# Low halves of the K and V weights: an accumulating DMA in place of a VectorE subtraction

## The chip, the cores and the metric

The kernel runs on one core of one Trainium2 chip. A core has TensorE (PE, matrix products), VectorE (DVE), ScalarE (ACT), GpSimd (POOL) and SyncE (SP), each with its own instruction stream, and 16 DMA engines that all queues share. The metric is the device time of one execution in microseconds. Three runs of the kernel before took 2151.91, 2154.38 and 2157.09 us; the median, 2154.38 us, is the time to compare with.

## The reference

One layer of a hybrid encoder over 256 tokens of width 2048, in float32:

```
h = x + W_out [ conv group || S5 group ] (rmsnorm(x))
h = h + MemCrossAttn(rmsnorm(h), rmsnorm(mem))      # 4 heads, 256 memory tokens
h = h + PEER(rmsnorm(h))                            # product-key experts
out = rmsnorm(h)

kv = (mem_n @ w_kv).reshape(bsz, 256, 2, 4, 512)    # w_kv is 2048 x 4096
k, v = kv[:, :, 0], kv[:, :, 1]
```

The change lies in the product with `w_kv`. Its first 2048 columns give K, the other 2048 give V.

## The kernel before

**How a weight product is made.** All large products go through one helper, `linear` (L146). It walks over blocks of 512 weight columns, and in each block over 8 tiles of 256 weight rows (`KG` = 2 groups of 128 rows). SP loads a tile of 512 KB into `w_raw` (L155). TensorE multiplies fast in the rounded format F32R, so each weight is taken apart into a high and a low half: ACT rounds the tile, `S.copy(hi, raw)` (L162), and DVE subtracts, `V.tensor_sub(lo, raw, hi)` (L163). TensorE then adds three products, high by high, high by low and low by high (L172 to L174 where tokens are the output rows, as for V; L181 to L183 where the output is transposed, as for K). For K this is 24 matmuls of 256 columns in a tile, for V 12 of 512 columns. The eighth tile of each block (`whole`) is not split: TensorE takes `w_raw` itself in float32 (L140, L143). So K and V have 64 tiles, 4 + 4 blocks of 8, and 56 of them are split.

**Buffers.** The pool `wp` has 5 buffers for `w_raw`, 3 for `w_hi` and 3 for `w_lo`. A buffer is used anew when its last reader is done, so a load waits for the split of the tile five before it, and a split waits for TensorE to be done with the tile three before it.

**What runs beside.** While K and V are made, the engines also run the S5 group (L428 to L469: table building on ACT, elementwise work and scans on DVE, small matmuls) and the depthwise convolution, 31 taps by 8 blocks of 128 channels, each tap one DVE instruction (L568). After V come the gated product of S5 (`ssm_glu_w`), the norms of the two groups and `w_out`.

**What sets the order.** Each engine runs its own stream strictly in order. The streams are laid out before the run by a scheduler that looks at priorities and at its own estimate of times: weight tiles are asked for `AHEAD` = 500 steps early and S5 bodies `S5_AHEAD` = 700 steps early, and the convolution fills the holes.

Of the kernel before, what the change touches and what calls it, by code (L numbers as in the profile page):

```python
# [9 lines left out]
F32 = mybir.dt.float32  # L10
# [4 lines left out]
AF = mybir.ActivationFunctionType  # L15
ALU = mybir.AluOpType
# [4 lines left out]
P = 128  # L21
T = 256
NTT = T // P
D = 2048
KT = D // P
# [3 lines left out]
PAD = CW - 1  # L29
KG = 2  # L30
AHEAD = 500
S5_AHEAD = 700
NPAIR = 32
NS = 64
# [26 lines left out]
W_IN, W_K, W_V = True, True, True  # L61
# [10 lines left out]
def trunk(ctx, tc, a, out, dbg=None):  # L72
    nc = tc.nc
    V, S, G, PE, SY = nc.vector, nc.scalar, nc.gpsimd, nc.tensor, nc.sync
# [45 lines left out]
    uctx = ctx.enter_context(ExitStack())  # L120
    with ExitStack() as wctx:
        atx = wctx.enter_context(ExitStack())
        wp = wctx.enter_context(tc.tile_pool(name="wp", bufs=3, side="right"))
        at = atx.enter_context(tc.tile_pool(name="at", bufs=1))
        psm = wctx.enter_context(tc.tile_pool(name="psm", bufs=3, space=PSUM))
        pst = wctx.enter_context(tc.tile_pool(name="pst", bufs=2, space=PSUM))
# [7 lines left out]
        def whole_matmuls(ps, x, raw, j, begin, end, rows_out):  # L134
            for i in range(KG):
                k = (j - (KT // KG - NWHOLE)) * KG + i
                first, last = begin and i == 0, end and i == KG - 1
                if rows_out:
                    for tt in range(NTT):
                        PE.matmul(ps[tt], x[:, k, tt * P:(tt + 1) * P], raw[:, i, :], start=first, stop=last)  # L140
                else:
                    for cb in range(4):
                        PE.matmul(ps[cb // 2][:, cb % 2, :], raw[:, i, cb * P:(cb + 1) * P], x[:, k, :],  # L143
                                  start=first and cb % 2 == 0, stop=last and cb % 2 == 1, skip_group_check=True)

        def linear(x, w, c0, ncol, evac, rows_out, kt=KT, korder=None, ahead=AHEAD, whole=None, cols=None):  # L146
            xh, xl = x
            js = korder or range(kt // KG)
            for n, (c, w_) in enumerate(cols or [(c, 512) for c in range(c0, c0 + ncol, 512)]):
                ncb = w_ // P  # L150
                ps = [psm.tile([P, 512] if rows_out else [P, 2, T], F32, name="mm", tag="mm") for _ in range(2)]
                for m, j in enumerate(js):
                    with tc.high_priority(offset=ahead):
                        raw = wp.tile([P, KG, w_], F32, name="w_raw", bufs=5)
                        SY.dma_start(raw, w[j * KG * P:(j + 1) * KG * P, c:c + w_].rearrange("(k p) c -> p k c", p=P))  # L155
                        full = whole is not None and j >= kt // KG - NWHOLE
                        if full:
                            whole_matmuls(ps, whole, raw, j, m == 0, m == len(js) - 1, rows_out)
                            continue
                        hi = wp.tile([P, KG, w_], F32R, name="w_hi")  # L160
                        lo = wp.tile([P, KG, w_], F32R, name="w_lo")
                        S.copy(hi, raw)  # L162
                        V.tensor_sub(lo, raw, hi.bitcast(F32))  # L163
                    for i in range(KG):
                        k = j * KG + i
                        first, last = m == 0 and i == 0, m == len(js) - 1 and i == KG - 1
                        ah, al = xh[k // 4][:, k % 4, :], xl[k // 4][:, k % 4, :]
                        if rows_out:
                            for tt in range(NTT):
                                o = ps[tt]  # L170
                                ts = slice(tt * P, (tt + 1) * P)
                                PE.matmul(o, ah[:, ts], hi[:, i, :], start=first, stop=False)  # L172
                                PE.matmul(o, ah[:, ts], lo[:, i, :], start=False, stop=False)  # L173
                                PE.matmul(o, al[:, ts], hi[:, i, :], start=False, stop=last)  # L174
                        else:
                            for cb in range(ncb):
                                o = ps[cb // 2][:, cb % 2, :]
                                end = cb % 2 == 1 or cb == ncb - 1
                                wh = hi[:, i, cb * P:(cb + 1) * P]
                                wl = lo[:, i, cb * P:(cb + 1) * P]  # L180
                                PE.matmul(o, wh, ah, start=first and cb % 2 == 0, stop=False, skip_group_check=True)  # L181
                                PE.matmul(o, wh, al, start=False, stop=False, skip_group_check=True)  # L182
                                PE.matmul(o, wl, ah, start=False, stop=last and end, skip_group_check=True)  # L183
                for half in range((ncb + 1) // 2):
                    evac(n, half, ps[half])
                yield n

        def run(g):
            for _ in g:
                pass  # L190
# [5 lines left out]
        with ExitStack() as mctx:  # L196
# [51 lines left out]
            def load_mem(src, gain):  # L248
                ssq = consts.tile([P, NTT, 4], F32, name="ssq_mem")
                x = act_tiles()  # L250
                xw = mp.tile([P, NWHOLE * KG, T], F32, name="x_whole")
                for n in range(4):
                    load_cols(src, None, ssq, n)
                r = row_rstd(ssq, "rstd_mem")
                for n in range(4):
                    xc, gb = load_cols(src, gain, None, n)
                    for tt in range(NTT):
                        V.scalar_tensor_tensor(xc[:, tt, :], xc[:, tt, :], r[:, tt:tt + 1], gb, op0=ALU.mult,
                                               op1=ALU.mult)
                    to_T(x, xw, n, xc)  # L260
                return x, xw

            def scaled(dst, ps, rb):
# [3 lines left out]

            uT = mp.tile([P, CQ, T], F32, name="uT")
            run(linear(xT, a["w_in"], 2 * CH, CH, lambda n, half, ps: V.tensor_mul(
                uT[:, 4 * n + 2 * half:4 * n + 2 * half + 2, :], ps, bc(rbx[:, None, :], [P, 2, T])), False, ahead=0))  # L270

# [201 lines left out]
            def s5_next():  # L473
                q = s5["q"]
                if q < CQ:
                  with tc.high_priority(offset=S5_AHEAD):
                    now = s5["tables"]
                    s5["tables"] = s5_tables(q + 1) if q + 1 < CQ else None
                    s5_body(q, now)
                    s5["q"] = q + 1  # L480

            for n in range(2):
                run(linear(xT, a["w_in"], n * 512, 512, ev_a(n), False, whole=xW if W_IN else None))
                s5_next()
                run(linear(xT, a["w_in"], CH + n * 512, 512, ev_g(n), False, whole=xW if W_IN else None))
                s5_next()
            memT, memW = load_mem(a["mem"], a["mem_norm_g"])
# [8 lines left out]
                S.copy(t, ps)  # L496
                SY.dma_start(v_dram[:, tt, 512 * n:512 * n + 512], t)

            for _ in linear(memT, a["w_kv_mem"], 0, D, ev_k, False, whole=memW if W_K else None):
                s5_next()  # L500
            kv_v = linear(memT, a["w_kv_mem"], D, D, ev_v, True, whole=memW if W_V else None)
            run(kv_v)
            for j in range(2):
                z = uT[:, 4 * j:4 * j + 4, :]
# [56 lines left out]
            for k in range(CW):  # L561
                for q in range(CQ):
                    src = cpad[:, q, k:k + T]
# [10 lines left out]
            for q in range(CQ):  # L574
                S.activation(acc[:, q, :], acc[:, q, :], AF.Silu, bias=colv[:, 2, q:q + 1],
                             scale=colv[:, 1, q:q + 1])
# [162 lines left out]
        for n in range((KD + 3) // 4):  # L739
            w = min(KD - 4 * n, 4)  # L740
# [384 lines left out]
```

## Time and profile before

| what | value |
|---|---|
| median of three runs | 2154.38 us |
| the profiled execution | 2160.26 us |
| its span in the trace | 2158.2 us |
| busy: PE, DVE, ACT, POOL | 92%, 82%, 48%, 35% of the span |
| K and V tiles | 64, of which 56 are split |

The profiled execution is 5.9 us longer than the median of the runs. The shares are averages over stages with different limits; what counts for this change is the stretch from about 220 to 460 us, in which K and V are made. Engine times in the trace are those of single instructions. PE's are modelled and overlap, so the pace of its matmuls is better read from how many stand in a stretch that it fills. A DMA has no line of its own in the table of instructions; its cost shows as the busy share of the 16 DMA engines and as pieces of the chain of waits.

### The profile page before, as it was taken

What the parts mean: (1) busy time and instruction counts of PE and PEld (TensorE: products, weight loads), DVE (VectorE), ACT (ScalarE), POOL (GpSimd) and SP (SyncE); (2) the same over time, 40 slices, a digit from 0 to 9 for tenths busy, and PEclk for the clock granted to TensorE, in tenths of its full rate; (3) what the DMA queues carried; (4) which work ended last, traced back from release to release, by engine and by line L of the source; (5) the groups of instructions that cost most, each with busy time, mean ns of one, the idle gap of its engine ahead of it and who ended that gap; (6) DMA issues with size and microseconds to landing.
All of it is one profiled execution on the core that took longest, in us unless ns stands there. A gap on an engine that the chain in (4) does not pass through costs nothing.

```text
span 2158.2 us, 31798 instructions
## 1 busy us (share of the span) xinstructions
PE 1985.0 (92%) x11459; PEld 1714.8 (79%) x11459; DVE 1778.4 (82%) x2905; ACT 1028.6 (48%) x1683; POOL 751.2 (35%) x548
## 2 busy tenths in 40 slices
PE   8998898999999999799999997888868999999997
PEld 7987786677799888788878886777656888888886
DVE  5789999977666557999976667788897999899997
ACT  5764454446445445233333322468794444444444
POOL 0000000000000003444456666332207877677773
PEclk9999899999999999899999998798999999999998
DMA  7654444554965568799999999987618999999995
GB/s 243 169 178 147 137 144 134 167 162 146 307 204 172 170 190 283 271 306 348 325 351 401 403 400 376 336 295 260 204 68 278 361 354 335 349 335 339 338 341 197
DMA packets 199133, 567.60 MB, mean 263 GB/s; under 512 B 31537, under 2 KB 36513, under 8 KB 198848
## 3 DMA queue, kind: packets, MB, share of 16 engines
q1 hardware_dynamic: 141632, 322.27, 45.5%
q0 software_dynamic: 57344, 243.30, 30.0%
q8 instruction: 90, 1.47, 0.3%
q14 instruction: 67, 0.55, 0.1%
HBM read 553.57 MB, written 11.93 MB: 262 GB/s over the span
## 4 chain that ended last, share of the span: by engine, by line
PE 45%; DVE 25%; issue 13%; DMA 8%; POOL 6%; ACT 3%; SPq 0%; POOLq 0%; ACTq 0%; DVEq 0%
PE acc L1073 7%; PE acc L1074 7%; PE acc L1072 7%; POOL u L859 5%; DVE u L861 5%; DVE acc L568 3%; DVE w_lo L163 3%; PE mm L183 3%; PE mm L181 3%; PE mm L182 3%; PE y L912 3%; PE mm L173 2%; PE mm L174 2%; PE mm L172 2%; DMA hnT<-ib_dram 1%
## 5 line engine op out<-in xcount | busy, mean ns | idle before, releaser
L861 DVE SCALAR_TENSOR_TENSOR u<-u,hnF 128x1280 f32<-128x1280 f32 x256 | 388.4, 1519 | 85.7 <-DMA u<-in_peer_u,uidx 84.3
L1037 POOL DMA_INDIRECT v<-in_peer_v,vidx x256 | 387.3, 1513 | 192.0 <-ACT WB L940 72.4
L859 POOL DMA_INDIRECT u<-in_peer_u,uidx x256 | 318.3, 1243 | 342.4 <-DVE u L861 259.6
L162 ACT CAST w_hi<-w_raw 128x1024 fp32r<-128x1024 f32 (+2 forms) x228 | 231.4, 1018 | 289.3 <-PE mm L182 128.6
L897 PE MATMUL sy<-hnT,ut 128*128 128x256 f32 x1536 | 353.4, 382 | 8.7 <-ACT ut L893 7.2
L163 DVE TENSOR_TENSOR w_lo<-w_raw,w_hi 128x1024 fp32r<-128x1024 f32 (+2 forms) x228 | 268.6, 1181 | 107.4 <-ACT w_hi L162 107.2
L897 PEld LDWEIGHTS sy<-hnT,ut 128*128 128x128 f32 x1536 | 284.9, 191 | 48.6 <-ACT ut L893 11.4
L103 ACT CAST vh<-vr 128x1472 fp32r<-128x1472 f32 x128 | 183.1, 1430 | 265.3 <-PE acc L1073 206.7
L1073 PE MATMUL acc<-vh,wl 128*128 128x512 f32 (+1 forms) x768 | 296.6, 386 | 5.0 <-DVE wl L1063 4.6
L183 PE MATMUL mm<-aT_hi,w_lo 128*128 128x256 f32 x960 | 272.3, 292 | 27.6 <-DVE w_lo L163 27.3
L1074 PE MATMUL acc<-vl,wh 128*128 128x512 f32 (+1 forms) x768 | 295.1, 386 | 0.0
L742 POOL TENSOR_TENSOR hnT<-aT_hi,aT_lo 128x1024 f32<-128x1024 f32 (+1 forms) x2 | 4.1, 2080 | 817.9 <-ACT w_hi L162 817.9
L181 PE MATMUL mm<-aT_hi,w_hi 128*128 128x256 f32 x960 | 277.0, 291 | 3.7 <-DVE sg L264 2.3
L1072 PE MATMUL acc<-vh,wh 128*128 128x512 f32 (+1 forms) x768 | 276.7, 385 | 3.5 <-ACT vh L103 2.5
L182 PE MATMUL mm<-aT_lo,w_hi 128*128 128x256 f32 x960 | 274.5, 288 | 0.0
L104 DVE TENSOR_TENSOR vl<-vr,vh 128x1472 fp32r<-128x1472 f32 x128 | 216.5, 1692 | 40.4 <-ACT vh L103 38.5
L1039 DVE SCALAR_TENSOR_TENSOR accg<-v,coef,accg 128x576 f32<-128x576 f32 x256 | 208.6, 815 | 11.0 <-DMA v<-in_peer_v,vidx 5.5
L183 PEld LDWEIGHTS mm<-aT_hi,w_lo 128*128 128x128 f32 x960 | 184.1, 196 | 35.9 <-DVE w_lo L163 32.9
L181 PEld LDWEIGHTS mm<-aT_hi,w_hi 128*128 128x128 f32 x960 | 186.6, 195 | 7.7 <-DVE sg L264 2.9
L182 PEld LDWEIGHTS mm<-aT_lo,w_hi 128*128 128x128 f32 x960 | 187.0, 195 | 1.3 <-issue 0.4
L893 ACT COPY ut<-ut 128x768 f32<-128x768 f32 x128 | 100.3, 801 | 168.7 <-PE ut L891 145.9
L1073 PEld LDWEIGHTS acc<-vh,wl 128*128 128x128 f32 x768 | 145.2, 189 | 36.3 <-DVE wl L1063 5.3
(335 smaller groups left out, 3426.2 us busy)
## 6 DMA issues: line engine op xcount, KB each, us to landing
vr<-in_peer_v SPq DMA_DIRECT2D x128, 736.0 KB
raw<-in_peer_u SPq DMA_DIRECT2D x128, 384.0 KB
w_raw<-in_w_kv_mem SPq DMA_DIRECT2D x64, 512.0 KB
w_raw<-in_w_in SPq DMA_DIRECT2D x48, 512.0 KB
w_raw<-in_w_out SPq DMA_DIRECT2D x32, 512.0 KB
w_raw<-in_w_q_mem SPq DMA_DIRECT2D x32, 512.0 KB
w_raw<-in_w_o_mem SPq DMA_DIRECT2D x32, 512.0 KB
hnT<-ib_dram SPq DMA_DIRECT2D x38, 256.0 KB
```

What stands on the lines that cost most here:

```text
L162: S.copy(hi, raw)
L163: V.tensor_sub(lo, raw, hi.bitcast(F32))
L181: PE.matmul(o, wh, ah, start=first and cb % 2 == 0, stop=False, skip_group_check=True)
L182: PE.matmul(o, wh, al, start=False, stop=False, skip_group_check=True)
L183: PE.matmul(o, wl, ah, start=False, stop=last and end, skip_group_check=True)
L859: G.indirect_dma_start(out=u, out_offset=None, in_=a["peer_u"].rearrange("e (q c) -> (e q) c", c=GU), in_offset=bass.IndirectOffsetOnAxis( ...
L861: V.scalar_tensor_tensor(u, u, 1.0, hnF[:, self.tt, :], op0=ALU.mult, op1=ALU.mult, accum_out=self.act[:, j:j + 1])
L897: PE.matmul(ps[:, b % 2, :], ut[:, k, :], hnT[:, k, :], start=k == 0 and b % 2 == 0, stop=k == KD - 1 and b % 2 == 1, skip_group_check=True)
L1037: G.indirect_dma_start(out=v, out_offset=None, in_=table, in_offset=bass.IndirectOffsetOnAxis(ap=vidx[tt][:, j:j + 1], axis=0))
L1072: PE.matmul(o, wh[:, tt, :], vh[:, cs_], start=b == 0, stop=False)
L1073: PE.matmul(o, wl[:, tt, :], vh[:, cs_], start=False, stop=False)
L1074: PE.matmul(o, wh[:, tt, :], vl[:, cs_], start=False, stop=b == NB - 1)
```

## The change

The split of K's and V's tiles gets another way to make the low half. ACT writes the negated weight, rounded to F32R, into `w_lo`, which is minus the high half. Then POOL starts a DMA that reads the same 512 KB of weights from HBM a second time and adds them to what stands in `w_lo`. The other products keep the subtraction on DVE. The 11 buffers of 4 KB in a partition are dealt out anew for all products: 3 for `w_raw` (before 5), 4 each for `w_hi` and `w_lo` (before 3).

```diff
+RAW_BUFS = 3
+HL_BUFS = 4
...
-        wp = wctx.enter_context(tc.tile_pool(name="wp", bufs=3, side="right"))
+        wp = wctx.enter_context(tc.tile_pool(name="wp", bufs=HL_BUFS, side="right"))
...
-                        raw = wp.tile([P, KG, w_], F32, name="w_raw", bufs=5)
-                        SY.dma_start(raw, w[j * KG * P:(j + 1) * KG * P, c:c + w_].rearrange("(k p) c -> p k c", p=P))
+                        raw = wp.tile([P, KG, w_], F32, name="w_raw", bufs=RAW_BUFS)
+                        src = w[j * KG * P:(j + 1) * KG * P, c:c + w_].rearrange("(k p) c -> p k c", p=P)
+                        SY.dma_start(raw, src)
...
                         S.copy(hi, raw)
-                        V.tensor_sub(lo, raw, hi.bitcast(F32))
+                        if dma_lo:
+                            S.activation(lo, raw, AF.Copy, scale=-1.0)
+                            G.dma_start(lo, src, accum_op=ALU.add)
+                        else:
+                            V.tensor_sub(lo, raw, hi.bitcast(F32))
...
-            for _ in linear(memT, a["w_kv_mem"], 0, D, ev_k, False, whole=memW if W_K else None):
+            for _ in linear(memT, a["w_kv_mem"], 0, D, ev_k, False, dma_lo=True, whole=memW if W_K else None):
                 s5_next()
-            kv_v = linear(memT, a["w_kv_mem"], D, D, ev_v, True, whole=memW if W_V else None)
+            kv_v = linear(memT, a["w_kv_mem"], D, D, ev_v, True, dma_lo=True, whole=memW if W_V else None)
```

Before, GpSimd's stream has nothing between the set-up constants at the start and the sum that makes `hnT`, some 800 us later:

```order
L97 IOTA part 128x1 x2
masks.py:199 AFFINE_SELECT ident<-ident 128x128
L357 IOTA par_i 128x1
L742 TENSOR_TENSOR hnT<-aT_hi_6954,aT_lo_6958 128x1024
L742 TENSOR_TENSOR hnT<-aT_hi_6955,aT_lo_6959 128x512
L804 TENSOR_TENSOR WB<-WB 128x256 x2
```

The same place on GpSimd after the change:

```order
L99 IOTA part 128x1 x2
masks.py:199 AFFINE_SELECT ident<-ident 128x128
L364 IOTA par_i 128x1
L168 DMA w_lo<-in_w_kv_mem 128x2x512 x56
L749 TENSOR_TENSOR hnT<-aT_hi_7010,aT_lo_7014 128x1024
L749 TENSOR_TENSOR hnT<-aT_hi_7011,aT_lo_7015 128x512
L811 TENSOR_TENSOR WB<-WB 128x256 x2
```

Fifty-six DMAs have come in, one for each split tile; nothing else stands between them.

On VectorE, one S5 table and body in the middle of K's tiles stood like this before (`sn`, `zr`, `zi` are tiles of S5, `acc` is the convolution):

```order
L420 TENSOR_TENSOR sn<-ph_w,sn 128x1024
L568 SCALAR_TENSOR_TENSOR acc<-cpad,cwT,acc 128x256
L163 TENSOR_TENSOR w_lo<-w_raw,w_hi 128x1024
L568 SCALAR_TENSOR_TENSOR acc<-cpad,cwT,acc 128x256 x4
L163 TENSOR_TENSOR w_lo<-w_raw,w_hi 128x1024
L450 TENSOR_TENSOR zr<-zr,t_2145 128x1024
L568 SCALAR_TENSOR_TENSOR acc<-cpad,cwT,acc 128x256
L451 TENSOR_TENSOR zi<-zi,t_2146 128x1024
L568 SCALAR_TENSOR_TENSOR acc<-cpad,cwT,acc 128x256
L163 TENSOR_TENSOR w_lo<-w_raw,w_hi 128x1024
L568 SCALAR_TENSOR_TENSOR acc<-cpad,cwT,acc 128x256
L421 TENSOR_SCALAR sn<-sn 128x1024
```

The same place on VectorE after the change:

```order
L427 TENSOR_TENSOR sn<-ph_w,sn 128x1024
L575 SCALAR_TENSOR_TENSOR acc<-cpad,cwT,acc 128x256 x7
L457 TENSOR_TENSOR zr<-zr,t_2145 128x1024
L458 TENSOR_TENSOR zi<-zi,t_2146 128x1024
L575 SCALAR_TENSOR_TENSOR acc<-cpad,cwT,acc 128x256
L428 TENSOR_SCALAR sn<-sn 128x1024
```

The subtractions are gone, and the pieces of the convolution stand side by side.

## Rows read from the trace of the kernel before

**Rows 1.** The page's 40 slices: busy tenths of DVE and of the DMA engines.

```profile
DVE  5789999977666557999976667788897999899997
...
DMA  7654444554965568799999999987618999999995
```

**Rows 2.** Busy time by stretch, five stretches around K and V.

```profile
core 0: us, PE busy (x) PEld busy (x) DVE busy (x) ACT busy (x) POOL busy (x), PEclk, DMA share, GB/s
140.00:220.00 80.00, 66.82 (x494) 61.61 (x494) 80.00 (x125) 44.17 (x63) 0.00 (x0) 0.90 0.48 148
220.00:340.00 120.00, 104.87 (x811) 93.29 (x811) 120.00 (x201) 56.96 (x81) 0.00 (x0) 0.95 0.48 141
340.00:460.00 120.00, 109.33 (x498) 76.91 (x497) 120.00 (x194) 47.77 (x58) 0.00 (x0) 0.96 0.52 156
460.00:540.00 80.00, 74.73 (x414) 62.57 (x413) 55.65 (x62) 45.54 (x52) 0.00 (x0) 0.96 0.46 150
540.00:600.00 60.00, 57.05 (x251) 44.52 (x250) 38.17 (x43) 28.64 (x39) 0.00 (x0) 1.00 0.94 312
```

**Rows 3.** Groups by line, 220 to 460 us: busy, mean ns, idle before.

```profile
L568 DVE SCALAR_TENSOR_TENSOR acc<-cpad,cwT,acc 128x256 f32<-128x256 f32 x201 | 84.8, 473 | 0.0
L163 DVE TENSOR_TENSOR w_lo<-w_raw,w_hi 128x1024 fp32r<-128x1024 f32 x53 | 64.1, 1211 | 0.0
...
L162 ACT CAST w_hi<-w_raw 128x1024 fp32r<-128x1024 f32 x53 | 55.4, 1047 | 85.8 <-PE mm L174 47.7 <-PE mm L182 34.8 <-DVE acc L568 1.8
```

**Rows 4.** Waits, 220 to 460 us: us in total, times, longest us.

```profile
PE mm L183 <- DVE w_lo L163: 14.0, 8, 5.4
...
PE mm L173 <- DVE w_lo L163: 9.0, 3, 4.6
```

**Rows 5.** Waits of SP's queue, 220 to 460 us.

```profile
SPq L155 <- DVE acc L568: 131.3, 34, 8.9
SPq L155 <- DVE w_lo L163: 58.3, 17, 8.3
```

**Rows 6.** DMA queues, 220 to 460 us: packets, MB, share of 16 engines.

```profile
q1 hardware_dynamic: 18502, 35.43, 49.4%
...
w_raw<-in_w_kv_mem SPq DMA_DIRECT2D x54, 512.0 KB
```

**Rows 7.** Busy time by stretch, two stretches that PE fills.

```profile
640.00:660.00 20.00, 20.00 (x170) 20.00 (x169) 12.70 (x14) 9.73 (x13) 0.00 (x0) 1.00 0.64 211
...
780.00:800.00 20.00, 20.00 (x91) 16.23 (x90) 12.08 (x13) 9.14 (x13) 0.00 (x0) 1.00 0.71 220
```

**Rows 8.** The chain that ended last: start us, us, what; 512 KB loads.

```profile
130.38 7.29 DMA xc<-in_mem
...
163.01 4.53 DMA xc<-in_mem
...
565.42 8.31 DMA w_raw<-in_w_out
...
578.02 9.19 DMA w_raw<-in_w_out
```

**Rows 9.** The page, groups by line: two kinds of DMA that POOL starts.

```profile
L1037 POOL DMA_INDIRECT v<-in_peer_v,vidx x256 | 387.3, 1513 | 192.0 <-ACT WB L940 72.4
L859 POOL DMA_INDIRECT u<-in_peer_u,uidx x256 | 318.3, 1243 | 342.4 <-DVE u L861 259.6
```

More of the change, by code (lines that the diff above doesn't have):

```diff
@@ L144, in whole_matmuls, with linear @@
                                   start=first and cb % 2 == 0, stop=last and cb % 2 == 1, skip_group_check=True)
-        def linear(x, w, c0, ncol, evac, rows_out, kt=KT, korder=None, ahead=AHEAD, whole=None, cols=None):
+        def linear(x, w, c0, ncol, evac, rows_out, kt=KT, korder=None, dma_lo=False, ahead=AHEAD, whole=None, cols=None):
             xh, xl = x
```

## The prediction

> **What bounds the kernel now.** I read the page's 40 slices first, to find the stretch that the change touches: DVE stands at 9 tenths or more in slices 3 to 8, while the DMA engines stand at 4 to 5 there [rows 1]. Then the busy times by stretch. From 140 to 460 us DVE is busy in every microsecond, 80 of 80, 120 of 120 and 120 of 120; in the 240 us of K and V (220 to 460) PE is busy 104.87 + 109.33 = 214.2 us, ACT 104.7 us, POOL not at all, and the DMA engines have half their time free [rows 2]. The groups by line say what fills DVE: convolution taps, 201 by 473 ns, and the low halves, 53 by 1211 ns, both with no idle time before them [rows 3]. The waits say what that costs PE: 14.0 + 9.0 = 23.0 us in which a matmul stood waiting for `w_lo` [rows 4], nearly all of PE's 240 − 214.2 = 25.8 us of idle time. SP's weight loads wait on DVE too, 131.3 + 58.3 us, because a `w_raw` buffer is only free when DVE has read it [rows 5]. So DVE ends last in this stretch, PE is only 11% behind it, and a faster DVE can win 25.8 us at the most before PE takes over.
>
> **What the change removes.** 56 subtractions by 1.211 us, 67.8 us of DVE [rows 3]. That is more than the 25.8 us that PE can give back. DVE falls to 240 − 67.8 = 172 us of work in this stretch and no longer decides.
>
> **What it adds on ACT.** 56 more passes over 128 x 1024 values; the cast of the same shape takes 1.047 us [rows 3], so 58.6 us. ACT's 104.7 us become 163 of 240, so it stays under PE. ACT works in order, and the copy of a finished K or V block and the S5 tables stand behind such a pass while it waits for a free `w_lo`; they have idle time of ACT around them, and I cost this at nothing.
>
> **What it adds on POOL.** 56 DMA starts on an engine that was idle. The trace has no plain start on POOL; an indirect start, which handles 128 rows, takes 1.243 or 1.513 us [rows 9]. The new one handles 128 x 2 runs of 512 values, so between 1.2 us and twice 1.513, 3.0 us: 70 to 169 us over 240, hidden beside PE. If each run cost two reads' worth of work it would be 6.1 us and 339 us, no longer hidden, and +99 us.
>
> **What it adds on the DMA engines.** This is the term that decides. Now the stretch moves 35.43 MB in 49.4% of the engines' time, 0.494 x 240 = 118.6 us of all 16 [rows 6], so 512 KB (0.524 MB) cost 0.524 / 35.43 x 118.6 = 1.76 us. No accumulating DMA is in the trace, so its cost has to be bounded. If the engines handle it as quickly as a load, it is 1.76 us, and 56 are 98 us: 118.6 + 98 = 217 us, within 240. But it has two inputs, the weights in HBM and what stands in `w_lo`, and one output. If each input costs what a load does, it is 3.51 us, and 56 are 197 us: 118.6 + 197 = 315 us, which does not fit into 240. Break-even is (240 − 118.6) / 56 = 2.17 us, only 1.24 times a load. I take 3.51 us, since reading 1 MB to write 512 KB is what the operation asks for: the stretch lasts 315 us instead of 240, +75 us. If the engines reach only the 0.94 that the fullest neighbouring stretch shows [rows 2], it is 315 / 0.94 = 335 us, +95 us. The upper end, an adder slower than the two reads, has no row near it; for the range I let the DMA cost up to three loads, 5.3 us: 118.6 + 295 = 414 us, +174 us.
>
> The Trainium skill, Collectives: The Full Stack, section "The bandwidth ceiling: the fold count and why AG ≠ RS ≠ AR", says that an add in the DMA engines costs nothing in itself but needs two source reads on the same ring, and gives 62.28 against 32.35 GB/s, 1.93 times. By it the DMA would be an estimated 1.93 x 1.76 = 3.4 us and the stretch 308 us, +68; by the lone row of the load it would be 217 us. No run here shows yet which holds.
>
> **The chain of one tile.** Before, the low half was ready 1.2 us after the high half, plus DVE's queue. Now it takes two ACT passes (2.1 us), a start (1.2 us) and a landing. Loads of 512 KB in the chain of waits took 4.53 and 7.29 us in half-full stretches and 8.31 and 9.19 us in the full one [rows 8]. PE's own part of a tile is 24 matmuls at 20 / 170 us, 2.8 us, for K, and 12 at 20 / 91 us, 2.6 us, for V [rows 7]. With four `w_lo` buffers a tile can be finished every (2.1 + 1.2 + 4.53 + 2.8) / 4 = 2.7 us at best and every (2.1 + 1.2 + 9.19 + 2.8) / 4 = 3.8 us at the landings of a full stretch. The pace now is 240 / 64 = 3.75 us. So even a transfer as cheap as a load leaves little margin once the engines are full.
>
> **The buffers of the other products.** A load used to run up to 5 + 3 = 8 tiles ahead of PE, now 3 + 4 = 7. Where loads are on the chain (540 to 600 us) a tile less is worth up to 2.6 us of PE at its end; in the stretch from 140 to 220, where PE idles 80 − 66.82 = 13.2 us [rows 2], a fourth split tile may win back some. I take these together as 0, with −10 to +5 in the range.
>
> **Sum.** The profiled execution takes 2160.3 us; +75 makes 2235. It stands 5.9 us above the median of the runs, so the forecast for the median is 2154.4 + 75 = 2229 us.
>
> **The rivals.**
> *The transfer is hidden.* The accumulating DMA costs about a load, the engines have room (217 of 240), the chain of a tile holds at 2.7 us, and PE's waits for `w_lo` go: −23.0 us, 2131. For it speaks that the DMA engines are half free now; against it, that two reads would have to cost as much as one, and that the last ten per cent of the engines come with landings of 8 to 9 us. Chance 0.20.
> *It is hidden, but the chain of a tile takes DVE's place.* Cost near a load, landings of 9.19 us: 56 tiles by 3.8 us and 8 whole ones at the present 3.75 us are 243 us in place of 240. No change, 2154 to 2158. Chance 0.08, of which I count 0.06 as no change and 0.02 as slower.
> *The DMA engines become the bound*, the forecast, 2229: slower from the point at which one accumulation costs more than 2.17 us of the 16 engines. Chance 0.62.
> *POOL or the adder is slower still*, so that a DMA costs more than three loads: above 2154 + 174 = 2328. At four loads, 7.0 us, it would be 118.6 + 393 − 240 = +272, 2426. Nothing in the trace speaks for it, nor excludes it. Chance 0.10.
> *The change does not do what it says* would be that the low half on DVE was no load on the path; the 23.0 us of waits exclude that.
>
> **How the numbers follow.** The likeliest case gives 2229, by itself 2190 (accumulations at 2.8 us) to 2328. The range has to reach into the hidden case, of which I leave its better half outside: 2140; above, 2320, which leaves out the slowest one. A run of this kernel can tell a change from none at about 0.2%, 4 us. Faster 0.20, within 0.2% 0.06, slower 0.02 + 0.62 + 0.10 = 0.74.
>
> **What would show it.** Right: in K's and V's stretch the DMA share stands above 0.9, DVE has holes, the stretch is about 315 us long, and the matmuls of L183 and L173 (L190 and L180 in the changed file) wait for the DMA into `w_lo`, not for DVE. The share divided among loads and accumulations gives some 3.5 us for one of the latter. Wrong: a DMA share that stays under 0.8 with PE busy 95%, which would be the hidden transfer, or a share that stays low while matmuls wait, which would be POOL's starts or the landing time; then the size of a start on POOL tells which.

## The result and the profile after

The changed kernel takes 2172.3 us (2171.7 to 2174.7) beside 2155.3 us (2151.9 to 2157.1) of the kernel before, ratio 1.0083 [1.0065, 1.0100]. It is slower, as forecast, but by 17 us and not by 75. The profiled execution spans 2170.5 us, before 2158.2.

The page's slices of the changed kernel, DVE and the DMA engines:

```profile
DVE  6899787656765557999976667678897999899997
...
DMA  7668999985865568799999999987617999999995
```

Against [rows 1] the two have changed places in slices 5 to 9 (217 to 488 us): the DMA engines stand at 9 and 8 tenths there, DVE at 7, 8, 7, 6 and 5. The busy times of the changed kernel in the five stretches of [rows 2]:

```profile
core 0: us, PE busy (x) PEld busy (x) DVE busy (x) ACT busy (x) POOL busy (x), PEclk, DMA share, GB/s
140.00:220.00 80.00, 67.52 (x500) 60.24 (x498) 74.58 (x124) 48.51 (x65) 9.89 (x8) 0.94 0.77 203
220.00:340.00 120.00, 105.76 (x758) 92.31 (x759) 94.54 (x184) 78.87 (x106) 30.14 (x25) 0.93 1.02 249
340.00:460.00 120.00, 103.41 (x460) 69.06 (x459) 86.98 (x152) 65.18 (x78) 27.75 (x24) 0.94 1.03 246
460.00:540.00 80.00, 77.87 (x443) 64.63 (x442) 46.61 (x47) 45.01 (x51) 0.00 (x0) 1.00 0.57 184
540.00:600.00 60.00, 56.25 (x248) 43.87 (x248) 42.73 (x51) 30.65 (x42) 0.00 (x0) 1.00 0.83 273
```

DVE has holes of 25.5 and 33.0 us in K's and V's stretches, the DMA share is 1.02 and 1.03 where it was 0.48 and 0.52, and the granted clock of PE is no better than before. The groups by line of the changed kernel, 220 to 460 us (columns as in [rows 3]):

```profile
L575 DVE SCALAR_TENSOR_TENSOR acc<-cpad,cwT,acc 128x256 f32<-128x256 f32 x197 | 82.5, 486 | 0.0
...
L165 ACT CAST w_hi<-w_raw 128x1024 fp32r<-128x1024 f32 x51 | 53.1, 1042 | 68.8 <-DMA w_raw<-in_w_kv_mem 45.8 <-PE mm L189 11.7 <-DMA w_raw<-in_ssm_glu_w 8.9
L167 ACT ACTIVATE w_lo<-w_raw 128x1024 fp32r<-128x1024 f32 x48 | 50.6, 1055 | 22.1 <-DMA w_raw<-in_w_kv_mem 19.7 <-PE mm L180 2.4
```

The pass added on ACT costs 1.055 us. ACT's longest idle time now ends with the landing of a raw tile (45.8 us), where [rows 3] had PE. The waits, 220 to 466 us (us in total, times, longest us), and the waits of SP's queue in the same stretch:

```profile
POOL w_lo L168 <- ACT w_lo L167: 147.1, 43, 12.1
ACT w_hi L165 <- DMA w_raw<-in_w_kv_mem: 45.8, 19, 6.2
...
PE mm L180 <- DMA w_lo<-in_w_kv_mem: 16.6, 13, 3.0
PE mm L190 <- DMA w_lo<-in_w_kv_mem: 14.7, 8, 6.7
```

```profile
SPq L158 <- DMA w_raw<-in_w_kv_mem: 67.7, 30, 7.7
SPq L158 <- ACT w_lo L167: 60.0, 27, 3.8
```

The matmuls wait for the DMA into `w_lo`, 16.6 + 14.7 = 31.3 us, in place of the 23.0 us for DVE [rows 4]; SP's queue no longer waits for DVE's convolution [rows 5] but for landings and ACT. POOL stands idle for ACT (147.1 us), so the rate of its starts is not the limit. The DMA queues, 200 to 440 us (packets, MB, share of 16 engines; q0 is POOL's queue), and the line of the new start:

```profile
q0 software_dynamic: 13483, 25.98, 60.9%
q1 hardware_dynamic: 17334, 33.19, 41.7%
```

```profile
L168 POOL DMA_DIRECT2D w_lo<-in_w_kv_mem x56: 1194/1203/1477, 183.4 to 447.5; - x56
...
DMA to landing us min/median/max: 6.7/9.3/13.1
```

25.98 MB are 49.6 transfers of 512 KB, in 0.609 x 240 = 146.2 us: 2.95 us of the 16 engines for one. A load costs 0.524 / 33.19 x 0.417 x 240 = 1.58 us here (1.76 us in half-full engines by [rows 6]). A start takes 1.20 us of POOL, the low end of the estimate from [rows 9].

How far each product has come is read from the last instruction of its tile. The copies of the finished K (first row) and V blocks, before and then after (ns min/median/max, first and last start us):

```profile
L491 ACT COPY kv_ev<-mm x8: 585/587/590, 234.3 to 339.0; 128x512 f32<-128x512 f32 x8
...
L496 ACT COPY kv_ev<-mm x8: 585/587/590, 372.0 to 457.8; 128x512 f32<-128x512 f32 x8
```

```profile
L498 ACT COPY kv_ev<-mm x8: 563/567/587, 236.1 to 333.8; 128x512 f32<-128x512 f32 x8
...
L503 ACT COPY kv_ev<-mm x8: 566/578/587, 360.7 to 465.3; 128x512 f32<-128x512 f32 x8
```

V ends 7.5 us later, and the gated product behind it (matmuls of `zh` with `w_lo`), which starts while V ends, 1.9 us earlier: 487.2 against 489.1. So K and V are worth almost nothing either way, and the 12.3 us between the two spans arise later. The ends of the products stand in the lines of the tile `mm`, before and then after: the last matmul of peer_w_q's product, the last of w_o_mem's, and the last weight load of the gated product:

```profile
L183 PE MATMUL mm<-aT_hi,w_lo x960: 274/283/581, 15.3 to 870.8; 128*128 128x256 f32 x192
...
L174 PE MATMUL mm<-w_hi,aT_lo x368: 389/397/632, 339.1 to 813.6; 128*128 128x512 f32 x184
...
L183 PEld LDWEIGHTS mm<-zh,w_lo x64: 186/188/333, 457.2 to 489.1; 128*128 128x128 f32 x64
```

```profile
L190 PE MATMUL mm<-aT_hi,w_lo x960: 274/283/583, 14.2 to 877.7; 128*128 128x256 f32 x192
...
L181 PE MATMUL mm<-w_hi,aT_lo x368: 391/397/632, 331.0 to 812.5; 128*128 128x512 f32 x184
...
L190 PEld LDWEIGHTS mm<-zh,w_lo x64: 186/188/188, 465.8 to 487.2; 128*128 128x128 f32 x64
```

In the table "GLU" is the end of the gated product (the start of its last weight load), "q" the length of peer_w_q's product from the end of the w_o_mem product, and "y" the length of the stretch in which `y` is made from `E` and `WA`, from the end of the `sy` matmuls; ends are read as the start of the last matmul. All are in us, of one profiled execution each. The ratio is of the timed runs, with its 95% interval.

| kernel | raw / hi / lo | last V copy | GLU | q | y | median | ratio |
|---|---|---|---|---|---|---|---|
| before | 5/3/3 | 457.8 | 489.1 | 57.2 | 98.2 | 2155.3 | |
| changed | 3/4/4 | 465.3 | 487.2 | 65.2 | 106.0 | 2172.3 | 1.0083 [1.0065, 1.0100] |
| e1 no accumulation | 3/4/4 | 458.1 | 488.0 | 65.8 | 102.9 | 2170.9 | 1.0077 [1.0059, 1.0096] |
| e2 old buffers | 5/3/3 | 488.1 | 509.7 | 57.4 | 104.3 | 2181.5 | 1.0119 [1.0099, 1.0139] |
| e3 nothing added | 5/3/3 | 421.2 | 443.8 | 58.1 | 104.9 | 2125.8 | 0.9863 [0.9844, 0.9881] |
| e4 plain DMA | 3/4/4 | 419.9 | 441.8 | 65.5 | 103.5 | 2125.3 | 0.9876 [0.9854, 0.9897] |
| e5 half accumulated | 5/3/3 | 457.8 | 487.9 | 58.1 | 94.4 | 2157.9 | 1.0006 [0.9991, 1.0022] |
| e6 subtraction on POOL | 5/3/3 | 515.3 | 537.9 | 57.9 | 96.6 | 2208.1 | 1.0244 [1.0230, 1.0258] |
| e7 five low | 3/3/5 | 484.3 | 506.9 | 68.8 | 98.7 | 2197.6 | 1.0201 [1.0178, 1.0224] |
| e8 four raw in peer_w_q | 3/4/4 | 467.6 | 489.5 | 57.3 | 106.3 | 2169.3 | 1.0068 [1.0051, 1.0085] |
| e9 e8, half accumulated | 3/4/4 | 453.8 | 487.6 | 55.9 | 99.9 | 2164.7 | 1.0041 [1.0026, 1.0055] |
| e10 e8, two of seven | 3/4/4 | 466.8 | 502.4 | 55.9 | 101.8 | 2172.7 | 1.0073 [1.0057, 1.0089] |
| e11 e8, V only | 3/4/4 | 467.5 | 489.4 | 57.3 | 110.3 | 2169.6 | 1.0054 [1.0037, 1.0072] |
| e12 changed, again | 3/4/4 | 467.9 | 489.8 | 65.3 | 101.8 | one run | |

### The profile page after: what moved, and what is told of

Read it like the earlier page. It is cut to its first block, busy times and chain, and to the rows that moved or that the text cites. A ratio compares the mean times of both kernels' runs of the same rounds, so it can differ in the third digit from the quotient of the medians.

```text
span 2170.5 us, 31893 instructions
## 1 busy us (share of the span) xinstructions
PE 1990.8 (92%) x11459; PEld 1713.5 (79%) x11459; DVE 1715.7 (79%) x2849; ACT 1078.6 (50%) x1739; POOL 805.3 (37%) x604
## 4 chain that ended last, share of the span: by engine, by line
PE 48%; issue 18%; DVE 15%; DMA 9%; POOL 8%; ACT 3%; SPq 0%; POOLq 0%; ACTq 0%; DVEq 0%
PE acc L1080 8%; PE acc L1081 8%; PE acc L1079 8%; POOL u L866 5%; DVE u L868 5%; PE mm L190 4%; PE mm L188 4%; PE mm L189 3%; PE y L919 3%; POOL w_lo L168 2%; PE mm L180 2%; PE mm L181 2%; PE mm L179 2%; DMA w_lo<-in_w_kv_mem 2%; DMA w_raw<-in_w_out 1%
## 5 line engine op out<-in xcount | busy, mean ns | idle before, releaser
L866 POOL DMA_INDIRECT u<-in_peer_u,uidx x256 | 301.5, 1178 | 371.3 <-DVE u L868 295.3
L170 DVE TENSOR_TENSOR w_lo<-w_raw,w_hi 128x1024 fp32r<-128x1024 f32 (+2 forms) x172 | 203.0, 1183 | 126.9 <-ACT w_hi L165 125.5
L190 PE MATMUL mm<-aT_hi,w_lo 128*128 128x256 f32 x960 | 276.7, 293 | 26.2 <-DMA w_lo<-in_w_kv_mem 20.2
L168 POOL DMA_DIRECT2D w_lo<-in_w_kv_mem x56 | 67.8, 1211 | 379.0 <-DVE acc L575 181.5
```

The source lines that it names most:

```text
L866: G.indirect_dma_start(out=u, out_offset=None, in_=a["peer_u"].rearrange("e (q c) -> (e q) c", c=GU), in_offset=bass.IndirectOffsetOnAxis( ...
```

## The experiments

**e1, the buffers alone.** The changed kernel without its new operand: DVE subtracts again.

```diff
-for _ in linear(memT, a["w_kv_mem"], 0, D, ev_k, False, dma_lo=True, whole=...):
+for _ in linear(memT, a["w_kv_mem"], 0, D, ev_k, False, whole=...):
```

(and the same for V)

> Only the buffers are dealt out as in the changed kernel (3 raw, 4 high, 4 low); K and V keep the subtraction on DVE. Theory A (the 17 us come after V: a weight product with 3 raw buffers loses in the last product, peer_w_q, and the order laid anew behind it costs the rest): slower than before by 5 to 17 us, last peer_w_q matmul some 7 us later than 870.8 us. Theory B (the full DMA engines of K's and V's stretch cost the time): within 4 us of before.

Measured: 1.0077, +16.6 us, with no accumulation in it, as theory A has it. The gated product ends at 488.0, nearly as before (489.1); peer_w_q takes 65.8 us, as in the changed kernel. The dealing of the buffers, which the prediction set to 0, brings the whole loss by itself.

**e2, the old buffers.** The accumulation with 5 raw, 3 high and 3 low tiles.

```diff
-RAW_BUFS = 3
-HL_BUFS = 4
+RAW_BUFS = 5
+HL_BUFS = 3
```

> The accumulating DMA with the buffers as before (5 raw, 3 high, 3 low). Theory A: the last peer_w_q matmul within 2 us of where the gated product's end puts it before, and the whole within 5 us of before (about 2155). Theory B: as slow as the changed kernel or slower, 2172 to 2190, since one low buffer less makes the wait for a landing of 9.3 us longer.

Measured: peer_w_q is back at 57.4 us, but the gated product ends at 509.7, 22 us later than with four high and four low tiles, and the whole is 1.0119, 2181.5 us, within what theory B said. So the accumulation loses more with three tiles than with four, and the fourth was bought from the raw tiles. Neither dealing serves both products.

**e3, nothing added.** As e2, without the start on POOL: the low halves of K and V are then −hi alone, so the transfers and the weight that they add are left out.

```diff
-                            G.dma_start(lo, src, accum_op=ALU.add)
```

> Buffers as before; in K and V ACT writes minus the high half as the low half and nothing is added to it: neither the subtraction on DVE nor the DMA. It leaves out the low half's value in K and V. Both theories: this is the most that taking the subtraction off DVE can give; V's last copy about 20 us before 457.8 us. If the gain arrives at the end, 2130 to 2138; if what follows V does not start earlier for it, 2150 to 2158.

Measured: 0.9863; the gated product ends 45.3 us earlier than before, at 443.8. The stretches of e3:

```profile
220.00:320.00 100.00, 100.00 (x793) 88.54 (x792) 98.12 (x193) 80.01 (x108) 0.00 (x0) 1.00 0.59 179
320.00:420.00 100.00, 100.00 (x492) 70.35 (x492) 85.17 (x148) 70.66 (x85) 0.00 (x0) 1.00 0.58 173
```

PE is never idle and its granted clock is 1.00. V's last copy starts 36.6 us earlier than before (421.2 against 457.8), where the expectation had some 20, and the whole is below its 2130 to 2138. So the subtractions were worth 36.6 us in K and V and 45 us by the end of the gated product, not the 25.8 us of idle time that [rows 2] shows.

**e4, a plain DMA.** The changed kernel with a copy in place of the accumulation: the low halves hold the whole weight, the sum is left out.

```diff
-                            G.dma_start(lo, src, accum_op=ALU.add)
+                            G.dma_start(lo, src)
```

> The changed kernel with the DMA copying the weights into the low half in place of adding them: one input in place of two. It leaves out the subtraction of the high half in K and V. If the second input is what an accumulation costs more, a DMA of POOL takes 1.5 to 1.8 us of the 16 engines in place of 2.95 and their share in 240 to 460 us falls from 1.03 to 0.7 to 0.85; V's last copy comes some 10 us before 465.3. Theory A: the whole still 5 to 12 us above before. Theory B: at or under before, 2145 to 2156.

Measured: 0.9876, the gated product at 441.8, earlier than either theory had it. So 56 starts on POOL, the ACT passes and the second transfer cost nothing against e3 (443.8), which has other buffers. The queues of e4, 200 to 440 us, its line of starts, and its two stretches:

```profile
q1 hardware_dynamic: 21160, 40.53, 51.7%
q0 software_dynamic: 14395, 27.75, 38.6%
```

```profile
L168 POOL DMA_DIRECT2D w_lo<-in_w_kv_mem x56: 700/703/913, 184.6 to 403.9; - x56
```

```profile
220.00:320.00 100.00, 98.76 (x748) 86.62 (x741) 92.32 (x183) 76.16 (x101) 16.85 (x24) 0.99 0.93 293
320.00:420.00 100.00, 99.44 (x488) 67.78 (x490) 85.28 (x146) 65.36 (x79) 15.45 (x22) 1.00 0.91 290
```

A plain transfer costs 0.386 x 240 / 27.75 x 0.524 = 1.75 us of the engines, the accumulating one 2.95 us, 1.69 times as much. Adding in place of copying takes the 45.4 us back (487.2 − 441.8). It costs more in three ways that e4 does not part: the engine time, the start on POOL (1.20 against 0.70 us), and the landing. By the packets of queue q0, the last packet of a transfer ends at the median 8.4 us after its start on POOL began in the changed kernel and 5.4 us in e4. Even 91 to 93% full engines leave PE at 99%; at 102 to 103% it waits.

**e5, half accumulated.** As e2, with every second tile on DVE (24 of 56 by DMA).

```diff
-                        if dma_lo:
+                        if dma_lo and j % 2:
```

> Buffers as before; only every second split tile of K and V (24 of 56) gets its low half by the accumulating DMA, the other 32 by DVE. Theory rate (the DMA engines' time for two inputs, 2.95 us each, is what K and V wait for): 24 x 2.95 = 71 us beside 119 us of other transfers fit into the stretch, DVE gives up 29 us, so the gated product ends 15 to 35 us before 489.1 and the whole is at 2125 to 2145. Theory landing (three low buffers are too few for a landing of some 9 us): waits for the landing remain, the gated product ends within 10 us of 489.1.

Measured: 1.0006 [0.9991, 1.0022], no change, the best of the versions that compute everything. The theory that only the rate of the engines counts wanted the gated product early; it ends at 487.9, as the landing theory said. The stretches and waits of e5 (200 to 460 us):

```profile
220.00:320.00 100.00, 85.95 (x664) 77.87 (x664) 91.56 (x162) 56.13 (x75) 10.82 (x9) 0.96 0.72 189
320.00:420.00 100.00, 89.61 (x467) 66.69 (x466) 92.31 (x159) 52.10 (x69) 10.86 (x9) 0.97 0.79 203
```

```profile
PE mm L190 <- DMA w_lo<-in_w_kv_mem: 21.9, 9, 4.5
...
PE mm L180 <- DMA w_lo<-in_w_kv_mem: 13.0, 9, 4.0
```

The engines are 72 and 79% busy and DVE 92%, and still the matmuls wait 34.9 us for landings. By the packets, the accumulations of e5 end 8.2 us after their start on POOL began (median), against 8.4 us in the changed kernel: with the engines a quarter empty they are hardly faster. So there is a second limit beside the rate of the engines, the time of one landing against the few tiles that may be under way.

**e6, the subtraction on POOL.** As e2, with the low halves of K and V subtracted on GpSimd.

```diff
-                            S.activation(lo, raw, AF.Copy, scale=-1.0)
-                            G.dma_start(lo, src, accum_op=ALU.add)
+                            G.tensor_sub(lo, raw, hi.bitcast(F32))
```

> Buffers as before; K and V's subtraction on GpSimd instead of DVE, no accumulating DMA. A sum of 128x1024 took GpSimd some 2.1 us (L742), 56 make 118 us of an idle engine. If taking the subtraction off DVE is all that is needed, the time comes near that without any subtraction (2125.8): 2125 to 2140, with peer_w_q's stretch at 57 to 58 us. In this program the stretch of the PEER settling is laid almost as before: theory order (the 5 to 8 us there come from the order laid anew) expects 98 to 100 us between the last dense product and the last y<-E,WA; without it 103 to 106.

Measured: 1.0244, the slowest. Groups of e6, 200 to 450 us:

```profile
L574 DVE SCALAR_TENSOR_TENSOR acc<-cpad,cwT,acc 128x256 f32<-128x256 f32 x196 | 129.1, 716 | 0.0
L167 POOL TENSOR_TENSOR w_lo<-w_raw,w_hi 128x1024 fp32r<-128x1024 f32 x45 | 128.3, 2870 | 128.2 <-ACT w_hi L165 110.0 <-PE mm L189 12.0 <-PE mm L188 6.1
```

The subtraction took 2.87 us on average, where the expectation had 2.1 us; that was the median of two shapes, and the sum of 128 x 1024 among them took 2.62 us. The subtraction left DVE, yet DVE stayed busy throughout: a convolution tap took 716 ns on average in place of 473 [rows 3] while POOL's subtraction ran beside it. The Trainium skill, SBUF — State Buffer, section "SBUF: two separate sides", says that VectorE with two SBUF inputs and a GpSimd operation that reads SBUF shut each other out of a shared pair of ports. The times of e6 agree with that; the expectation had not reckoned with it. The expectation's second question, on the y stretch, is taken up below: it lasts 96.6 us here.

**e7, five low tiles.** The changed kernel with 3 high and 5 low tiles.

```diff
-HL_BUFS = 4
+HL_BUFS = 3
...
-                        lo = wp.tile([P, KG, w_], F32R, name="w_lo")
+                        lo = wp.tile([P, KG, w_], F32R, name="w_lo", bufs=5)
```

> The accumulating DMA with 3 raw, 3 high and 5 low buffers. Theory rate: V's last copy within 6 us of 465.3, since the engines are already full. Theory landing: a fifth buffer brings V's last copy 10 to 20 us forward, as the fourth did (488.1 to 465.3).

Measured: 1.0201, the gated product at 506.9, beside 509.7 of e2. Both theories missed. A tile holds a high and a low buffer until its matmuls are over, so the smaller of the two numbers should be the depth, and that is three again; the time agrees with that reading. Five high and five low tiles beside three raw ones would be 13 buffers where 11 are dealt out; no run has them.

**e8, four raw tiles in peer_w_q.** That product has no DMA of its own for the low half; its raw tiles take the four `w_lo` buffers and its low tiles the three `w_raw` ones.

```diff
+            r_tag, l_tag = ("w_lo", "w_raw") if cols else ("w_raw", "w_lo")
...
-                        lo = wp.tile([P, KG, w_], F32R, name="w_lo")
+                        lo = wp.tile([P, KG, w_], F32R, name="w_lo", tag=l_tag, bufs=...)
```

(and the raw tile with `r_tag`)

> The changed kernel, but in the last weight product (peer_w_q) the raw tiles go through the four buffers of the low halves and the low halves through the three raw ones. Theory (peer_w_q loses 8 us because 3 raw buffers let too few loads run ahead): its stretch falls from 65.2 us to 58 to 62, the whole from 2172 to 2165 to 2169. If it is the order of the loads or something else, it stays at 64 to 66.

Measured: peer_w_q takes 57.3 us. So the cause of its 8 us is that three raw buffers are too few there; four are enough. The wait in question in the changed kernel, 812 to 878 us, and in e8, 815 to 881 us:

```profile
ACT w_hi L165 <- DMA w_raw<-in_peer_w_q: 19.1, 12, 3.7
```

```profile
ACT w_hi L166 <- DMA w_raw<-in_peer_w_q: 11.1, 6, 4.0
```

The kernel before has no such wait there. The whole came out at 1.0068, 2169.3 us and only 3 us under the changed kernel; in the profiled execution the y stretch stayed long (106.3 us) and the gated product ended 2.3 us later.

**e9, e10 and e11, mixtures on e8.** By DMA go the tiles of odd `j` (24 of 56), those of `j` 2 and 5 (16), and those of V alone (28).

```diff
-                        if dma_lo:
+                        if dma_lo and j % 2:          # e9
+                        if dma_lo and j in (2, 5):    # e10
+                        if dma_lo and rows_out:       # e11
```

> Every second split tile of K and V (24 of 56) by the accumulating DMA, with 3 raw, 4 high and 4 low buffers and the exchange of buffers in peer_w_q of the run before. Theory: with all 56 the DMA engines were the limit (share 1.0), with 24 on three low buffers the landing was; four buffers and 24 DMAs leave both behind: share in 220 to 420 us at 0.7 to 0.8, waits of matmuls for the landing under 12 us (34.9 with three buffers), the gated product's end at 455 to 475 us (before 489.1), the whole 2130 to 2148. If the landing still ends last, the gated product stays at 484 to 492 and the whole at 2155 to 2170.

> As the half run with four buffers, but only two of seven split tiles (16 of 56) by the accumulating DMA. DVE gives up 16 x 1.21 = 19 us, and nothing else is near its limit: the gated product ends 10 to 20 us before 489.1, the whole at 2138 to 2152. Slower than the run with 24 if the landing is hidden there, faster if not.

> The accumulating DMA for V alone (28 of 56, one after the other), buffers as in the two runs beside it. Theory: within V's stretch the engines are as full as with all 56 (share near 1.0 there, under 0.6 in K's), so V's part of the time is that of the changed kernel and K's that of before: the gated product ends within 8 us of 487, the whole 2155 to 2172.

Measured: 1.0041, 1.0073 and 1.0054. In e9 the second case of its expectation came out, in e10 neither: at shares of 0.63 to 0.75 the matmuls still wait for landings, 35.7 us (e9) and 46.3 us (e10), and e10, with fewer accumulations, is the slower of the two, where its expectation had it faster if landings still show. The fourth low tile took nothing from the 34.9 us of e5. With it came three raw tiles in place of five, and ACT's rounding pass waits 55.4 us (e9) and 47.4 us (e10) for raw tiles to land (220 to 460 us), which it doesn't do in e5; there it waits for matmuls to free a tile, 32.1 + 21.3 us. So the mixtures are short of tiles in one pool or the other; no run here has enough of all three. e11 did what was expected. Its stretches:

```profile
220.00:320.00 100.00, 84.65 (x642) 76.16 (x641) 100.00 (x168) 45.72 (x63) 0.00 (x0) 0.93 0.44 134
320.00:420.00 100.00, 82.19 (x386) 56.93 (x385) 82.50 (x155) 60.66 (x78) 25.61 (x21) 0.97 0.99 242
```

K with DVE full, V with the DMA engines full: two limits in one kernel, and the same end.

**e12, the changed kernel once more**, for a second profile of the y stretch.

> The changed kernel unaltered, for a second profile of it, to see whether the 106.0 us of the stretch in which 'y' is made from 'E' and 'WA' (98.2 us before) belong to the kernel or to one execution. Theory A (the kernel's own order of instructions sets it): again 104 to 108 us, PE's wait for 'hit' there again 22 to 26 us, and the stretch of peer_w_q again 64 to 66 us. Theory B (it varies from one execution to the next as the spread of the other kernels, 94 to 110 us): it comes out anywhere in 95 to 110 us, most likely nearer to 101, with the wait for 'hit' moving along. The whole, by both, 2170 to 2176 us.

Measured: 2166.5 us in one run beside 2158.4 us of the kernel before, under the 2170 to 2176 us of both theories. peer_w_q again takes 65.3 us. The matmuls of the y stretch, before, changed, and changed again:

```profile
L912 PE MATMUL y<-E,WA x256: 321/383/587, 1326.9 to 1424.3; 128*128 128x128 f32 x128
```

```profile
L919 PE MATMUL y<-E,WA x256: 319/423/587, 1331.9 to 1437.0; 128*128 128x128 f32 x128
```

```profile
L919 PE MATMUL y<-E,WA x256: 321/422/586, 1334.3 to 1435.3; 128*128 128x128 f32 x128
```

From the end of `sy` it is 98.2, 106.0 and 101.8 us. Some 4 us of the 7.8 vary from one execution to the next, as theory B has it; the wait for `hit` (23.1 us) stays where theory A has it.

## Why the prediction was right and wrong

**Right: the mechanism in K and V.** The bound went from DVE to the DMA, with a share above 0.9, holes on DVE and matmuls waiting for the DMA into `w_lo`. Whether the rate of its engines or the landings set the pace is open (see the rival of the tile's chain below). ACT's passes and a start on POOL for each tile are hidden: e4 has both (its starts take 0.70 us), and its gated product ends 47.3 us earlier than before.

**Right by luck: "slower".** K and V, in which the forecast put the loss, end the gated product 1.9 us earlier. The buffers alone lose as much as the whole change (e1, 1.0077 against 1.0083), and that term stood in the forecast as 0.

**Wrong: the +75 us, the term of the DMA engines.** It came out near nothing. Three sizes are wrong in "118.6 + 197 = 315 us, which does not fit into 240". An accumulation costs 2.95 us, not 3.51; it is 1.69 plain transfers, where two full reads would make 2. That alone leaves 118.6 + 56 x 2.95 = 284 us. A load in full engines costs 1.58 us, so the other traffic of [rows 6] is 35.43 / 0.524 x 1.58 = 107 us, not 118.6. And the work isn't held in the 240 us: the starts run from 183.4 us, 8 of them before 220. With these it is 107 + 48 x 2.95 = 248 us, at a share of 1.02 to 1.03 some 242. The K and V copies show 465.3 − 236.1 = 229.2 us beside 223.5 before, +5.7. The rule of the Trainium skill that the forecast weighed (Collectives: The Full Stack, section "The bandwidth ceiling: the fold count and why AG ≠ RS ≠ AR", two source reads on one ring, 1.93 times) has the right direction; the runs show 1.69, and the measurement decides.

**Wrong: "a faster DVE can win 25.8 us at the most before PE takes over."** e3 won 36.6 us at V's last copy and 45.3 us at the end of the gated product. PE's 214.2 us of busy time [rows 2] were at a granted clock of 0.95 and 0.96; with DVE out of the way it is 1.00, the level of 2.4 GHz throughout. The low clock of the kernel before stands at some of PE's waits for `w_lo`. One of 5.4 us ends at 265.2 us, and the two pieces of 5 us around it show (columns as in [rows 2]):

```profile
260.00:265.00 5.00, 0.00 (x0) 0.00 (x0) 5.00 (x8) 2.36 (x3) 0.00 (x0) 0.69 0.00 0
265.00:270.00 5.00, 4.84 (x21) 4.62 (x22) 5.00 (x10) 0.00 (x0) 0.00 (x0) 0.63 0.63 209
```

Another of 4.6 us ends at 365.9 us, and from 365 to 370 us the clock is 0.50, the level of 1.2 GHz. An estimate from [rows 2]: at full clock the 214.2 us are 0.95 x 104.87 + 0.96 x 109.33 = 204.6 us, 9.6 less, and 25.8 + 9.6 = 35.4 us, close to the 36.6. So by this estimate the clock is most of what the 25.8 us left out up to there; the other 8.7 us of the 45.3 come behind V's last copy. Time that PE is busy at a lowered clock isn't all work that it needs. This ceiling doesn't stand in the sum of 2229, but it does in the rival of the hidden transfer: that one had 2131, and e4, whose transfer costs about a load, takes 2125.3. By the ends of the gated product, K and V come to −45.3 us for the subtractions (e3), −2.0 for the starts, the plain transfers and the new buffers (e4 against e3), and +45.4 for adding in place of copying: −1.9 in all.

**Wrong: "I take these together as 0", the buffers of the other products.** By e1 this term, with what follows from it, is the 17 us. Only a part is traced to its place. Of the 12.3 us between the two spans, 8.0 are peer_w_q's; e1 shows them without the accumulation, e2 takes them away with five raw tiles, e8 with four. That is shown. Another 7.8 are the y stretch's, which stays open below, and the rest of the span gives 3.5 back. The other 4.7 of the 17 us are no part of the two spans: the profiled execution of the kernel before was 5.0 us longer than its median, and that of the changed kernel is its median. The prediction had the mechanism, loads that run fewer tiles ahead, but looked for it at 540 to 600 us, where nothing is lost: from the end of the gated product to that of w_o_mem's it is 325.3 us after, 324.5 before. The loss lies at 812 to 878 us, where ACT waits 12 times for a raw tile, 19.1 us together, and the bound of +5 was too small for it.

**Open: the y stretch**, 3.6 to 7.8 us. There PE waits for `hit` from DVE. The wait in the kernel before and in the changed one, over the stretch (us in total, times, longest us):

```profile
PE more L922 <- DVE hit L920: 17.0, 11, 9.0
```

```profile
PE more L929 <- DVE hit L927: 24.6, 19, 9.0
```

Over the kernels of the table the stretch is by and large the longer the longer this wait: 14.2 us in e5 (94.4), 17.8 in e9 (99.9), 23.5 in e2 (104.3), 27.9 in e11 (110.3). The granted clock by and large falls with it, 0.86 in e5, 0.77 before, 0.71 in the changed kernel, 0.70 in e11. No edit touches that code, but the scheduler laid its order anew: between the two events that bound the stretch PE has 497 matmuls before and 505 in the changed kernel. The six kernels with 497 or 498 (before, e2, e5, e6, e9, e10) take 94.4 to 104.3 us, the eight with 505 or 506 take 98.7 to 110.3. So the order goes with a part of it, but either group spreads over some 10 us, and one and the same kernel took 106.0 and 101.8. No run moved the order alone, so how much is order and how much chance isn't settled. It also limits what a version like e8 could give back.

**The rival of the tile's chain** is not excluded. The mixtures e5, e9 and e10 wait for landings with engines a fifth or more empty. In the changed kernel the rival's own sum, with the measured landing (9.3 us, which holds the start), is (2.1 + 9.3 + 2.8) / 4 = 3.55 us, and 56 tiles by 3.55 and 8 by 3.75 are 229 us; the copies show 229.2, and the sum of the DMA engines gives 242 of 240. Both fit. For the engines speaks their share of 1.02 and 1.03; against it, that pieces of 5 us reach 1.10 and 1.11, so that some room may be left, and that the landing is as long in less full engines (8.4 us by the packets in e10, at shares of 0.63 and 0.64). e4 relieves both at once. A run with the same transfers and more than four tiles in every pool would part them; there is none. The forecast gave this rival 0.08.

Two slips in the reading change nothing: DVE's nines in [rows 1] stand in slices 4 to 8, and 0.524 / 35.43 x 118.6 is 1.75, not 1.76.

## What to carry to other kernels

Where an engine is relieved, ask what the next one does at its full clock: a busy share at a granted clock under 1.00 overstates its work. A DMA with two inputs is costed at its engine time, and then its landing time is held against the number of tiles that can be under way; by e2 and e7 that is the smallest of the pools that a tile holds. Buffers taken from a shared pool are paid for where another product runs on them, so that product's stretch is priced before the one that is being changed.

## What the runs showed of the hardware

- An accumulating transfer of 512 KB from HBM into SBUF took 2.95 us of the 16 DMA engines, a plain one from the same queue 1.75 us; its start took 1.20 us of POOL, the plain one's 0.70 us. It landed after 6.7, 9.3 and 13.1 us (least, median, most). By its packets it was as slow where the engines were less full: 8.4 us at shares of 1.01 to 1.06 (the changed kernel), 8.2 at 0.72 to 0.79 (e5), 8.4 at 0.63 and 0.64 (e10), medians; the plain one took 5.4 us at 0.91 to 0.93 (e4).
- DMA shares over 1.00 occur (1.02 and 1.03 over 120 us): the packets' times overlap, so a share of 1.00 isn't a hard ceiling of the sum.
- A subtraction of 128 x 1024 values took 2.87 us on average on POOL beside 1.21 us on DVE, and DVE's own work became slower beside it, the tap 716 against 473 ns (e6).
